# Rotary position embedding on one core: stores widened by ScalarE and issued by SyncE in place of casting stores from the software queue

## The chip, the cores and the metric

The kernel runs on 1 core of one Trainium2 chip. The metric is device time in microseconds for one launch; each kernel is run several times and the median is given. The engines named here are VectorE (DVE in the profile), ScalarE (ACT), GpSimd (POOL) and SyncE (SP). TensorE does nothing in this kernel. DMAs that GpSimd issues go through the software queue (q0 in the profile, "software_dynamic"); DMAs that SyncE issues go through a hardware queue (q1, "hardware_dynamic"). Both queues are served by the same 16 DMA engines of the core.

## The reference

```python
# x: (8, 2048, 16, 64) float32: batch, sequence, heads, head dimension
# cos, sin: (2048, 32) float32
x1, x2 = x[..., :32], x[..., 32:]
out1 = x1 * cos - x2 * sin
out2 = x1 * sin + x2 * cos
out = concatenate([out1, out2], axis=-1)      # float32
```

The cosines and sines depend on the position in the sequence alone and are shared by all batches and heads. The input and the output have 67.1 MB each. There are three multiplications or additions for each element of the output, so the kernel moves much and computes little.

## The kernel before

**Tiling.** A batch has 2048 positions. They are laid over 128 partitions, J = 16 consecutive positions to a partition, so that a partition holds 16 x 1024 elements of a batch: 64 KB of consecutive float32 in HBM. On the chip a batch is kept as float16, 32 KB a partition, in a tile `xt`. Five such tiles exist (`NBUF = 5`, line 27). There is one scratch tile `v` of the same size (line 31).

**Loads and stores.** `load` (lines 49 to 57) issues one DMA from GpSimd for a whole batch; it reads float32 and writes float16, so the DMA engines do the cast. `store` (lines 59 to 63) issues one DMA from GpSimd for a whole batch, which reads float16 and writes float32. Loads and stores of all batches therefore stand in one queue, and that queue is worked off in the order in which GpSimd issues them.

**The rotation.** `rotate` (lines 65 to 81) runs three VectorE operations over rows j0 to j1 of a batch. The first multiplies the halves of each head in exchanged order by the sines, of which the first half is negated, into `v` (line 73). The second multiplies `xt` by the cosines in place (line 79). The third adds `v` to `xt` in place (line 81). All operands are float16.

**The start.** Rows 0 and 1 of batch 0 (`JA = 2`) take another way: SyncE loads them as float32 into the tile `head` (line 36), and ScalarE narrows them into `xt` (line 84). SyncE then loads the sines and the cosines (lines 44 and 45). ScalarE turns them into float16 tables (lines 88 to 90). GpSimd issues the loads of batches 0 to 3 (line 83). Rows 0 and 1 are rotated first, and a store of row 0 alone (line 102, through line 100) goes out before the load of batch 4 (line 109). The order of these in the queue is fixed by hand with the `add_manual_dep` calls.

**The loop** (lines 116 to 128). For each batch, VectorE rotates the whole batch; GpSimd then issues its store, and then the load of the batch five further on, which first waits until the store has left the buffer.

**The end** (lines 129 to 147). The last batch is stored in three parts. Rows 0 to 8 go by the software queue (the DMA called `gate`, line 130), rows 9 to 13 too (line 132). Rows 14 and 15 are widened to float32 by ScalarE into `head` (line 140), and SyncE stores them (line 141) when `gate` has landed.

Of the kernel before, what the change touches and what calls it, by code (L numbers as in the profile page):

```python
# [1 line left out]

# [4 lines left out]


@with_exitstack  # L10
def kernel(
    ctx: ExitStack,
    tc: tile.TileContext,
    x: bass.AP,
    cos: bass.AP,
    sin: bass.AP,
    out: bass.AP,
):
    nc = tc.nc
    f16 = mybir.dt.float16  # L20
    f32 = mybir.dt.float32

    B, S, H, D = x.shape
    Dh = D // 2
    P = nc.NUM_PARTITIONS
    J = S // P
    NBUF = 5

    const_pool = ctx.enter_context(tc.tile_pool(name="rope_const", bufs=1))
    io_pool = ctx.enter_context(tc.tile_pool(name="rope_io", bufs=NBUF))  # L30
    tmp_pool = ctx.enter_context(tc.tile_pool(name="rope_tmp", bufs=1))

    JA = 2
    head = const_pool.tile([P, JA, H, D], f32)
    x0 = x[0].rearrange("(p j) h d -> p j (h d)", j=J)
    nc.sync.dma_start(  # L36
        out=head.rearrange("p j h d -> p (j h d)"),
        in_=x0[:, 0:JA, :].rearrange("p j f -> p (j f)"),
    )
    sin_f = const_pool.tile([P, J, Dh], f32)  # L40
    cos_f = const_pool.tile([P, J, Dh], f32)
    cos_h = const_pool.tile([P, J, Dh], f16)
    sin_h = const_pool.tile([P, J, D], f16)
    nc.sync.dma_start(out=sin_f, in_=sin.rearrange("(p j) d -> p j d", j=J))  # L44
    nc.sync.dma_start(out=cos_f, in_=cos.rearrange("(p j) d -> p j d", j=J))

    loads = []

    def load(b):
        xt = io_pool.tile([P, J, H, D], f16)  # L50
        j0 = JA if b == 0 else 0
        dma = nc.gpsimd.dma_start(  # L52
            out=xt[:, j0:J, :, :].rearrange("p j h d -> p (j h d)"),
            in_=x[b].rearrange("(p j) h d -> p j (h d)", j=J)[:, j0:J, :].rearrange("p j f -> p (j f)"),
        )
        loads.append(dma)
        return xt

    def store(b, xt, j0=0):
        return nc.gpsimd.dma_start(  # L60
            out=out[b].rearrange("(p j) h d -> p j (h d)", j=J)[:, j0:J, :].rearrange("p j f -> p (j f)"),
            in_=xt[:, j0:J, :, :].rearrange("p j h d -> p (j h d)"),
        )

    def rotate(xt, j0, j1):
        v = tmp_pool.tile([P, J, H, D], f16)
        n = j1 - j0
        js = slice(j0, j1)
        shape = [P, n, H, 2, Dh]
        sin_b = sin_h[:, js, :].rearrange("p j (e d) -> p j e d", e=2).unsqueeze(2).to_broadcast(shape)  # L70
        cos_b = cos_h[:, js, :].unsqueeze(2).to_broadcast([P, n, 2 * H, Dh])
        xe = xt[:, js, :, :].rearrange("p j h (e d) -> p j h e d", e=2)
        nc.vector.tensor_mul(  # L73
            out=v[:, js, :, :].rearrange("p j h (e d) -> p j h e d", e=2),
            in0=xe[:, :, :, ::-1, :],
            in1=sin_b,
        )
        xw = xt[:, js, :, :].rearrange("p j h (e d) -> p j (h e) d", d=Dh)
        nc.vector.tensor_mul(out=xw, in0=xw, in1=cos_b)  # L79
        xa = xt[:, js, :, :].rearrange("p j h d -> p (j h d)")  # L80
        nc.vector.tensor_add(out=xa, in0=xa, in1=v[:, js, :, :].rearrange("p j h d -> p (j h d)"))  # L81

    tiles = [load(b) for b in range(NBUF - 1)]
    nc.scalar.copy(  # L84
        out=tiles[0][:, 0:JA, :, :].rearrange("p j h d -> p (j h d)"),
        in_=head.rearrange("p j h d -> p (j h d)"),
    )
    nc.scalar.copy(out=sin_h[:, :, Dh:D], in_=sin_f)  # L88
    nc.scalar.mul(out=sin_h[:, :, 0:Dh], in_=sin_f, mul=-1.0)  # L89
    nc.scalar.copy(out=cos_h, in_=cos_f)  # L90
    rotate(tiles[0], 0, JA)
    def part(b, j0, j1):
        return (
            out[b].rearrange("(p j) h d -> p j (h d)", j=J)[:, j0:j1, :].rearrange("p j f -> p (j f)"),
            tiles[b][:, j0:j1, :, :].rearrange("p j h d -> p (j h d)"),
        )

    def store_rows(b, j0, j1):
        dst, src = part(b, j0, j1)
        return nc.gpsimd.dma_start(out=dst, in_=src)  # L100

    first = store_rows(0, 0, 1)
    tc.add_manual_dep(
        first.ins,
        loads[NBUF - 2].ins.name,
        mybir.DependencyInfo(mybir.DependencyClass.NoSync, mybir.DependencyReason.DATA),
        reason="order of the ring",
    )
    tiles.append(load(NBUF - 1))
    tc.add_manual_dep(  # L110
        loads[NBUF - 1].ins,
        first.ins.name,
        mybir.DependencyInfo(mybir.DependencyClass.NoSync, mybir.DependencyReason.DATA),
        reason="order of the ring",
    )
    for b in range(B):
        rotate(tiles[b], JA if b == 0 else 0, J)
        if b < B - 1:
            st = store(b, tiles[b], 1 if b == 0 else 0)
            if b == 0:  # L120
                tc.add_manual_dep(
                    st.ins,
                    first.ins.name,
                    mybir.DependencyInfo(mybir.DependencyClass.NoSync, mybir.DependencyReason.DATA),
                    reason="order of the ring",
                )
        if b + NBUF < B:
            tiles.append(load(b + NBUF))
    dst, src = part(B - 1, 0, 9)
    gate = nc.gpsimd.dma_start(out=dst, in_=src)  # L130
    dst, src = part(B - 1, 9, J - JA)
    rest = nc.gpsimd.dma_start(out=dst, in_=src)  # L132
    tc.add_manual_dep(
        rest.ins,
        gate.ins.name,
        mybir.DependencyInfo(mybir.DependencyClass.NoSync, mybir.DependencyReason.DATA),
        reason="order of the ring",
    )
    dst, src = part(B - 1, J - JA, J)
    nc.scalar.copy(out=head.rearrange("p j h d -> p (j h d)"), in_=src)  # L140
    end = nc.sync.dma_start(out=dst, in_=head.rearrange("p j h d -> p (j h d)"))
    tc.add_manual_dep(
        end.ins,
        gate.ins.name,
        mybir.DependencyInfo(mybir.DependencyClass.Sync, mybir.DependencyReason.DATA),
        reason="the last rows go out behind this part",
    )


# [1 line left out]
_INS = ['x', 'cos', 'sin']  # L151
_OUTS = [((8, 2048, 16, 64), 'float32')]


# [23 lines left out]
```

## Time and profile before

| What | Value |
|---|---|
| median of 3 runs | 316.88 us (316.84 to 317.36) |
| span of the profiled execution | 315.7 us |
| own time of the profiled execution | not listed; the median of the runs is 1.2 us above the span |
| VectorE busy | 209.1 us (66%), 27 instructions |
| ScalarE busy | 6.8 us (2%), 6 instructions |
| GpSimd busy | 9.9 us (3%), 22 instructions |
| software queue q0 | 2592 packets, 99.09 MB, 98.1% of 16 engines' span |
| hardware queue q1 | 576 packets, 2.62 MB, 2.3% |
| HBM read and written | 67.63 MB and 67.11 MB |
| a load of a full batch, issue to landing | 41.3 us (median of 7) |

How to read it: busy time is summed over the instructions of an engine; the share is that of the span. For a DMA queue, the share is the time that its packets took, over the span of all 16 DMA engines. A packet here is one row of one partition, and its size in the records is that of the side that is written: a full batch is 128 packets of 64 KB when it is stored and 128 packets of 32 KB when it is loaded. Each of the 16 engines moves 8 of the 128 rows. The time from issue to landing holds the waiting in the queue as well as the transfer. The trace also records each packet by itself, with its start, its duration and its queue; the text calls these the packet records.

The profile has a row of digits for the DMA engines, one for each fortieth of the span, where 9 means busy for 90% or more. The view by stretches gives, for a stretch of time, what each engine was busy, the DMA share and the GB/s written.

### The profile page before, as it was taken

How to read it: one execution, taken by the hardware profiler on the slowest of the kernel's cores; microseconds unless marked ns; L12 is line 12 of the kernel's file. 1: busy time of each engine (PE TensorE's matmuls, PEld its weight loads, DVE VectorE, ACT ScalarE, POOL GpSimd, SP SyncE). 2: the span in 40 equal slices, each digit the busy share in tenths (PEclk: the TensorE clock that was granted, in tenths of full speed). 3: DMA queues.
4: the chain of work that ended last, by engine and by line, in shares of the span. 5: the costliest groups of instructions: out<-in, count | busy, mean ns of one | idle time of the engine just before them, and what ended most of it. 6: DMA issues, size and time to landing. Idle time of an engine off the chain costs nothing.

```text
span 315.7 us, 122 instructions
## 1 busy us (share of the span) xinstructions
DVE 209.1 (66%) x27; ACT 6.8 (2%) x6; POOL 9.9 (3%) x22
## 2 busy tenths in 40 slices
DVE  0010699999999999999999999994009994000000
ACT  4100000000000000000000000000000002000000
POOL 3000100000000000001000000100000001000000
DMA  9899999999999989999999999999999999999998
GB/s 277 183 262 208 199 220 245 199 199 199 266 199 199 498 374 523 399 332 241 224 199 199 390 407 399 399 531 266 199 249 482 399 399 515 415 399 399 432 434 330
DMA packets 3168, 101.71 MB, mean 322 GB/s; under 512 B 352, under 2 KB 352, under 8 KB 736
## 3 DMA queue, kind: packets, MB, share of 16 engines
q0 software_dynamic: 2592, 99.09, 98.1%
q1 hardware_dynamic: 576, 2.62, 2.3%
HBM read 67.63 MB, written 67.11 MB: 427 GB/s over the span
## 4 chain that ended last, share of the span: by engine, by line
DVE 25%; DMA 22%; issue 18%; another core or an unknown queue 17%; POOL 1%; ACT 1%; SPq 0%; POOLq 0%; DVEq 0%; ACTq 0%
DMA xt<-in_x_dram 12%; DMA cos_f<-in_cos_dram 10%; DVE xt L79 8%; DVE xt L81 8%; DVE v L73 8%; ACT head L140 1%; POOL out_dram L60 1%; POOL xt L52 0%; ACT cos_h L90 0%; SPq L44 0%; SPq L36 0%; POOLq L52 0%; POOLq L60 0%; DVEq L73 0%
## 5 line engine op out<-in xcount | busy, mean ns | idle before, releaser
L73 DVE TENSOR_TENSOR v<-xt,sin_h 128x16384 f16<-128x16384 f16 (+2 forms) x9 | 69.7, 7744 | 36.8 <-DMA xt<-in_x_dram 20.7
L79 DVE TENSOR_TENSOR xt<-xt,cos_h 128x16384 f16<-128x16384 f16 (+2 forms) x9 | 69.7, 7744 | 17.5 <-ACT cos_h L90 17.2
L81 DVE TENSOR_TENSOR xt<-xt,v 128x16384 f16<-128x16384 f16 (+2 forms) x9 | 69.7, 7744 | 0.3
L52 POOL DMA_DIRECT2D xt<-in_x_dram x8 | 4.4, 557 | 111.1 <-DMA out_dram<-xt 110.3
L140 ACT CAST head<-xt 128x2048 f32<-128x2048 f16 x1 | 1.9, 1897 | 229.5 <-DVE xt L81 229.5
L60 POOL DMA_DIRECT2D out_dram<-xt x7 | 3.7, 535 | 63.9 <-DVE xt L81 63.9
L130 POOL DMA_DIRECT2D out_dram<-xt x1 | 0.5, 531 | 46.3 <-DVE xt L81 46.3
L84 ACT CAST xt<-head 128x2048 f16<-128x2048 f32 x1 | 1.9, 1897 | 3.6 <-DMA head<-in_x_dram 3.6
L100 POOL DMA_DIRECT2D out_dram<-xt x1 | 0.5, 541 | 33.5 <-DVE xt L81 33.5
L84 ACT ACT_TABLE_LOAD x1 | 1.3, 1283 | 0.7 <-PEq L162 0.7
L90 ACT CAST cos_h<-cos_f 128x512 f16<-128x512 f32 x1 | 0.6, 618 | 17.8 <-DMA cos_f<-in_cos_dram 17.8
L88 ACT CAST sin_h<-sin_f 128x512 f16<-128x512 f32 x1 | 0.6, 617 | 7.2 <-DMA sin_f<-in_sin_dram 7.2
L89 ACT ACTIVATE sin_h<-sin_f 128x512 f16<-128x512 f32 x1 | 0.6, 624 | 0.0
L132 POOL DMA_DIRECT2D out_dram<-xt x1 | 0.5, 531 | 0.0
L162 POOL MEMSET const-float32-0.0<- 128x1 f32 x1 | 0.1, 99 | 0.2 <-issue 0.2
L162 POOL MEMSET const-bfloat16-1.0<- 128x1 bf16 x1 | 0.1, 102 | 0.0
L162 POOL MEMSET const-float32-1.0<- 128x1 f32 x1 | 0.1, 99 | 0.0
L162 POOL MEMSET const-uint8-127<- 128x1 uint8 x1 | 0.1, 99 | 0.0
## 6 DMA issues: line engine op xcount, KB each, us to landing
xt<-in_x_dram POOLq DMA_DIRECT2D x7, 4096.0 KB, 41.3
out_dram<-xt POOLq DMA_DIRECT2D x1, 7680.0 KB, 61.6
out_dram<-xt POOLq DMA_DIRECT2D x1, 4608.0 KB, 42.4
xt<-in_x_dram POOLq DMA_DIRECT2D x1, 3584.0 KB, 22.3
out_dram<-xt POOLq DMA_DIRECT2D x1, 2560.0 KB, 47.9
head<-in_x_dram SPq DMA_DIRECT2D x1, 1024.0 KB, 4.8
out_dram<-head SPq DMA_DIRECT2D x1, 1024.0 KB, 8.4
out_dram<-xt POOLq DMA_DIRECT2D x1, 512.0 KB, 47.1
```

Source lines behind the costliest of these rows:

```text
L52: dma = nc.gpsimd.dma_start(out=xt[:, j0:J, :, :].rearrange("p j h d -> p (j h d)"), in_=x[b].rearrange("(p j) h d -> p j (h d)", j=J)[:, ...
L60: return nc.gpsimd.dma_start(out=out[b].rearrange("(p j) h d -> p j (h d)", j=J)[:, j0:J, :].rearrange("p j f -> p (j f)"), in_=xt[:, j0:J ...
L73: nc.vector.tensor_mul(out=v[:, js, :, :].rearrange("p j h (e d) -> p j h e d", e=2), in0=xe[:, :, :, ::-1, :], in1=sin_b,)
L79: nc.vector.tensor_mul(out=xw, in0=xw, in1=cos_b)
L81: nc.vector.tensor_add(out=xa, in0=xa, in1=v[:, js, :, :].rearrange("p j h d -> p (j h d)"))
L84: nc.scalar.copy(out=tiles[0][:, 0:JA, :, :].rearrange("p j h d -> p (j h d)"), in_=head.rearrange("p j h d -> p (j h d)"),)
L88: nc.scalar.copy(out=sin_h[:, :, Dh:D], in_=sin_f)
L89: nc.scalar.mul(out=sin_h[:, :, 0:Dh], in_=sin_f, mul=-1.0)
L90: nc.scalar.copy(out=cos_h, in_=cos_f)
L100: return nc.gpsimd.dma_start(out=dst, in_=src)
L130: gate = nc.gpsimd.dma_start(out=dst, in_=src)
L140: nc.scalar.copy(out=head.rearrange("p j h d -> p (j h d)"), in_=src)
```

## The change

Every store now goes the way of the last two rows before. The batch is cut into four quarters of four positions to a partition (`JQ = 4`, 4096 elements a partition). For each quarter VectorE runs the same three operations, with a scratch tile `v` of a quarter's size, of which there are two. ScalarE then copies the quarter from float16 into one of three float32 tiles `stage` (16 KB a partition), and SyncE stores that tile, 2 MB, with no cast in the DMA. A widening waits until the store of three quarters before has landed.

There are four batch buffers, not five. The loads stay on the software queue as they were, and they are the only DMAs there. The load of batch b + 4 is issued after the loop over the quarters of batch b, and it waits until ScalarE has read the last quarter of that batch.

The small first rotation of two rows, the store of row 0 ahead of the others, the split of the last batch in three parts, and all orders given by hand are gone. Rows 0 and 1 of batch 0 are still loaded by SyncE, now into the first `stage` tile, and narrowed by ScalarE; they are rotated with the rest of the first quarter.

```diff
-    NBUF = 5
+    NBUF = 4
+    JA = 2
+    JQ = 4
...
-    tmp_pool = ctx.enter_context(tc.tile_pool(name="rope_tmp", bufs=1))
+    tmp_pool = ctx.enter_context(tc.tile_pool(name="rope_tmp", bufs=2))
+    out_pool = ctx.enter_context(tc.tile_pool(name="rope_out", bufs=3))
...
+    stage = out_pool.tile([P, JQ, H, D], f32, name="stage")
+    head = stage[:, 0:JA, :, :]
+    nc.sync.dma_start(out=flat(head), in_=rows(x, 0, 0, JA))
...
-    def store(b, xt, j0=0):
-        return nc.gpsimd.dma_start(
...
-    rotate(tiles[0], 0, JA)
...
-    first = store_rows(0, 0, 1)
...
     for b in range(B):
-        rotate(tiles[b], JA if b == 0 else 0, J)
-        if b < B - 1:
-            st = store(b, tiles[b], 1 if b == 0 else 0)
...
+        xt = tiles[b]
+        for j0 in range(0, J, JQ):
+            js = slice(j0, j0 + JQ)
+            v = tmp_pool.tile([P, JQ, H, D], f16, name="v")
...
+            nc.vector.tensor_mul(out=xw, in0=xw, in1=cos_b)
+            xa = flat(xt[:, js, :, :])
+            nc.vector.tensor_add(out=xa, in0=xa, in1=flat(v))
+            stage = out_pool.tile([P, JQ, H, D], f32, name="stage")
+            nc.scalar.copy(out=flat(stage), in_=xa)
+            nc.sync.dma_start(out=rows(out, b, j0, j0 + JQ), in_=flat(stage))
         if b + NBUF < B:
             tiles.append(load(b + NBUF))
-    dst, src = part(B - 1, 0, 9)
-    gate = nc.gpsimd.dma_start(out=dst, in_=src)
...
-    nc.scalar.copy(out=head.rearrange("p j h d -> p (j h d)"), in_=src)
-    end = nc.sync.dma_start(out=dst, in_=head.rearrange("p j h d -> p (j h d)"))
```

Here `rows(t, b, j0, j1)` is the slice of rows j0 to j1 of batch b in HBM with one run of consecutive elements to a partition, and `flat(t)` is a tile seen as one run to a partition.

More of the change, by code (lines that the diff above doesn't have):

```diff
@@ L26, with rows, flat @@
     J = S // P
-    NBUF = 5
+    NBUF = 4
+    JA = 2
+    JQ = 4
     const_pool = ctx.enter_context(tc.tile_pool(name="rope_const", bufs=1))
     io_pool = ctx.enter_context(tc.tile_pool(name="rope_io", bufs=NBUF))
-    tmp_pool = ctx.enter_context(tc.tile_pool(name="rope_tmp", bufs=1))
[L33 to L39, printed above, removed]
+    tmp_pool = ctx.enter_context(tc.tile_pool(name="rope_tmp", bufs=2))
+    out_pool = ctx.enter_context(tc.tile_pool(name="rope_out", bufs=3))
+    def rows(t, b, j0, j1):
+        return t[b].rearrange("(p j) h d -> p j (h d)", j=J)[:, j0:j1, :].rearrange("p j f -> p (j f)")
+    def flat(t):
+        return t.rearrange("p j h d -> p (j h d)")
+    stage = out_pool.tile([P, JQ, H, D], f32, name="stage")
+    head = stage[:, 0:JA, :, :]
+    nc.sync.dma_start(out=flat(head), in_=rows(x, 0, 0, JA))
     sin_f = const_pool.tile([P, J, Dh], f32)
@@ L45 @@
     nc.sync.dma_start(out=cos_f, in_=cos.rearrange("(p j) d -> p j d", j=J))
-    loads = []
     def load(b):
-        xt = io_pool.tile([P, J, H, D], f16)
+        xt = io_pool.tile([P, J, H, D], f16, name="xt")
         j0 = JA if b == 0 else 0
[L52 to L56, printed above, removed]
-        return xt
-    def store(b, xt, j0=0):
-        return nc.gpsimd.dma_start(
[L61 to L87, printed above, removed]
+        nc.gpsimd.dma_start(out=flat(xt[:, j0:J, :, :]), in_=rows(x, b, j0, J))
+        return xt
+    tiles = [load(b) for b in range(NBUF)]
+    nc.scalar.copy(out=flat(tiles[0][:, 0:JA, :, :]), in_=flat(head))
     nc.scalar.copy(out=sin_h[:, :, Dh:D], in_=sin_f)
@@ L90 @@
     nc.scalar.copy(out=cos_h, in_=cos_f)
-    rotate(tiles[0], 0, JA)
[L92 to L100, printed above, removed]
-    first = store_rows(0, 0, 1)
[L103 to L115, printed above, removed]
-    for b in range(B):
-        rotate(tiles[b], JA if b == 0 else 0, J)
-        if b < B - 1:
-            st = store(b, tiles[b], 1 if b == 0 else 0)
[L120 to L126, printed above, removed]
+    for b in range(B):
+        xt = tiles[b]
+        for j0 in range(0, J, JQ):
+            js = slice(j0, j0 + JQ)
+            v = tmp_pool.tile([P, JQ, H, D], f16, name="v")
+            sin_b = (
+                sin_h[:, js, :]
+                .rearrange("p j (e d) -> p j e d", e=2)
+                .unsqueeze(2)
+                .to_broadcast([P, JQ, H, 2, Dh])
+            )
+            cos_b = cos_h[:, js, :].unsqueeze(2).to_broadcast([P, JQ, 2 * H, Dh])
+            xe = xt[:, js, :, :].rearrange("p j h (e d) -> p j h e d", e=2)
+            xw = xt[:, js, :, :].rearrange("p j h (e d) -> p j (h e) d", d=Dh)
+            nc.vector.tensor_mul(
+                out=v.rearrange("p j h (e d) -> p j h e d", e=2),
+                in0=xe[:, :, :, ::-1, :],
+                in1=sin_b,
+            )
+            nc.vector.tensor_mul(out=xw, in0=xw, in1=cos_b)
[4 more added lines that the diff above has]
+            nc.sync.dma_start(out=rows(out, b, j0, j0 + JQ), in_=flat(stage))
@@ L127 @@
         if b + NBUF < B:
             tiles.append(load(b + NBUF))
-    dst, src = part(B - 1, 0, 9)
-    gate = nc.gpsimd.dma_start(out=dst, in_=src)
[L131 to L140, printed above, removed]
@@ L141 @@
-    end = nc.sync.dma_start(out=dst, in_=head.rearrange("p j h d -> p (j h d)"))
[L142 to L147, printed above, removed]
 _INS = ['x', 'cos', 'sin']
```

## The prediction

> **What bounds the kernel now.** I read the page's transfer part first, because the kernel moves 134.7 MB and computes little.
>
> ```profile
> DMA  9899999999999989999999999999999999999998
> ...
> q0 software_dynamic: 2592, 99.09, 98.1%
> ...
> HBM read 67.63 MB, written 67.11 MB: 427 GB/s over the span
> ```
>
> The DMA engines are 90% busy or more in every slice but three, and the software queue's packets alone fill 98.1% of 16 engines' span. No idle time is left to remove. VectorE's 66% lies beneath. So a change matters only if it alters the engines' work, or if it leaves them empty. The stretches by stage say what one byte costs:
>
> ```profile
> core 0: us, DVE busy (x) ACT busy (x) POOL busy (x), PEclk, DMA share, GB/s
> ...
> 104.00:140.00 36.00, 35.86 (x5) 0.00 (x0) 0.53 (x1) 1.00 0.99 424
> 142.00:178.00 36.00, 35.86 (x5) 0.00 (x0) 1.20 (x3) 1.00 1.01 218
> ```
>
> The first stretch is stores alone, the second loads alone. GB/s counts what is written: a load writes float16, so 218 means 436 read. Either way the float32 side limits. The packet records agree: a full batch, load or store, takes 19.32 us (8 rows of 64 KB on each engine, 2.415 us a row). Then the groups by shape, for the engines that get new work:
>
> ```profile
> L73 DVE TENSOR_TENSOR v<-xt,sin_h 128x16384 f16<-128x16384 f16 x7 | 60.8, 8693 | 20.9 <-DMA xt<-in_x_dram 20.7
> ...
> L140 ACT CAST head<-xt 128x2048 f32<-128x2048 f16 x1 | 1.9, 1897 | 229.5 <-DVE xt L81 229.5
> ...
> L73 DVE TENSOR_TENSOR v<-xt,sin_h 128x2048 f16<-128x2048 f16 x1 | 1.2, 1224 | 15.9 <-ACT sin_h L89 15.9
> ...
> L88 ACT CAST sin_h<-sin_f 128x512 f16<-128x512 f32 x1 | 0.6, 617 | 7.2 <-DMA sin_f<-in_sin_dram 7.2
> ```
>
> **New compute, all beneath the transfers.** A quarter is 4096 elements a partition. VectorE: (8693-1224)/14336 = 0.521 ns per element, so 1224 + 2048 x 0.521 = 2291 ns; three operations with 0.02 us between are 6.93 us a quarter, 27.7 a batch (26.2 before). ScalarE: (1897-617)/1536 = 0.833 ns per element, 3.60 us a widening. A quarter's store is a quarter of 19.32, about 4.85 us; with its share of loads the engines need 9.7 us a quarter. Thus VectorE (6.93) and ScalarE (3.60) are faster than the transfers on average; neither adds to the sum while quarters wait in line.
>
> **Does the line run empty?** Three widened quarters can stand at SyncE's queue. VectorE never waits for them: it works in the batch buffer and has two v. Only ScalarE waits, for the store three quarters back; behind that wait stand the next widenings, SP's next store, and, for a batch's last quarter, POOL's load into that buffer. Nothing but loads stands on POOL. First 43 us: as before; batches land at 23 and 43, cos at 33.6, VectorE starts its second operation at 34.3, and the first widened quarter leaves at about 42.5. Then the two queues share. How, the cos rows show (stretch 6 to 31 us):
>
> ```profile
> q0 software_dynamic: 192, 5.31, 98.6%
> q1 hardware_dynamic: 189, 0.33, 4.0%
> ```
>
> Small table rows of q1 went one at a time between big load rows, never several in a turn. If store rows (16 KB) take turns with load rows (64 KB), one quarter goes out per batch that comes in, in 8 x (2.41 + 0.61) = 24 us. Loads land at about 66, 90 and 114; then load 5 waits for quarter 7's widening, so for store 4: about 156, 195, 234. Each time one or more quarters are waiting, so the engines stay full. At 234 some 16 stores are left, 78 us, while VectorE ends near 262 and the last store starts near 309: 47 us of cover. Fewer buffers cost nothing there: the load that comes later leaves the engines to a store. If SP's rows were served only after all load rows waiting, batches would land earlier and the sum would be the same.
>
> **The sum, against the profiled execution.** Its span is 315.7; its own time is not listed, so I put it at the median, 316.88, which is 1.2 above the span.
> - Removed and added store rows. Before, the last store (8 KB rows, float32 on both sides, SP's queue) took 0.306 us a row by its packet records, 26.8 GB/s an engine; the casting row runs at 27.2. For a 16 KB row that gives 0.603 (as the casting row) to 0.612 (two 8 KB rows); I take 0.607, a fixed piece per row. 256 rows an engine, about +0.9 (0 to +2.3).
> - Alternation. A 2 KB row between two load rows stretched the pitch from 2.086 to 2.204, 0.118, where it takes 0.080 among its like: +0.038 for the two turns. About 48 of 64 load rows get a store row beside them: +1.8 (0 to +3.6, as a store row's turn does not appear).
> - Semaphore rows: 35 DMAs of SP at 0.009 to 0.022, for some ten stores at 0.042 in q0: +0.2 (0 to +0.4).
> - The first 512 KB store goes. The load ahead of it, batch 3, lasted 20.04 rather than 19.32: -0.7 (0 to -1.2).
> - The head: SP issues the same three loads, POOL four loads, ScalarE the same four operations; the small rotation of two rows goes, but batch 0 lands before cos: 0. The tail: both kernels end on SP's store with engines full until then: 0.
> - No q0 store is issued from POOL any more (0.54 us each): hidden, 0. The loads' issue may be slow beside VectorE: 20 us of delay would change nothing, as the queued stores and the 47 us cover it.
>
> Sum +2.2: 319.1 us, +0.7%. About 0.2%, 0.6 us, can be told from no change.
>
> A rule that speaks against the change: the Trainium skill, "DMA: Bandwidth & Descriptors", section "Anatomy of one DMA — SWDGE (gpsimd) path", fits each DMA on the software path as about 2.0 us fixed plus its bytes at 436 GB/s. Were that paid singly by some 22 more DMAs the estimate would be 44 us more, 361. This trace shows full batches following each other at 19.32 us with no such gap while another was queued; so I leave it out.
>
> **Rivals.**
> 1. *Three buffers are too few* (slower). The views of issues and of stretch 306.8 to 311.4 speak for it:
>
> ```profile
> out_dram<-head SPq DMA_DIRECT2D x1, 1024.0 KB, 8.4
> ...
> q0 software_dynamic: 96, 1.97, 103.4%
> ```
>
> SP's store was issued at 306.43 and no q1 row moved in that stretch; 8 x 0.306 = 2.45 of the 8.4 is transfer, 5.95 is waiting. I think it stood behind rows of q0 already taken up; at the start q1's first row came 1.45 us after SP's issue, with q0 empty. If the wait were each store's own, one turn of a buffer is (3.60 + w + 4.86)/3 against 4.86: it decides from w = 6.1, just above 5.95. At 7.4, 0.43 us on each of some 22 stores with no load beside them: +9.5 on the forecast, 328.
> 2. *SP's rows get more turns* (slower). The last batch still needs 27.7 + 3.6 + 1.5 + 4.9 + 0.4, 38 us after its landing; beyond about 279 it sets the end. That needs five store rows per load row (landing near 290, end 328 of span): about 329. The cos rows speak against it.
> 3. *Not slower: a store row passes beside a load row.* A load row writes only half of what it reads, so the engine's write side is half idle in it. If some of the inserted 0.607 is hidden, the 48 insertions turn: the other terms, +0.4, are gone from 0.01 us hidden each. A third hidden: -0.2 x 48 = -10, with +0.4, 307; all hidden, 288. Against it: the new store reads as many bytes as it writes, so a read side that a load fills has no room for it; and the 2 KB rows cost more than their own time beside a load, not less. They write as the load does, though; a store row writes the other way, which no row here shows.
> 4. *Reading and writing HBM at once slows both.* From 43 us on some 145 us of mixed rows; at 3%, +4.4: 323.5. Before never mixes for long; its switches between load and store batches show no loss.
>
> **How the numbers follow.** Forecast 0.53 (own range 316.3 to 322); rival 1: 0.10; 2: 0.04; 3: 0.21; 4: 0.12. Faster: most of rival 3, 0.18. Within 0.2%: rest of rival 3 and the low end of the forecast, 0.12. Slower: 0.70. The range from 311 to 328 takes in the bounds of the terms, the start of rival 3, rival 4 and rival 1's example; its deeper cases are left out.
>
> **What would show it.** Right: DMA digits of 9 throughout; q0 near half its share; VectorE's work ended by about 262, ScalarE waiting mostly for stores; widenings near 3.6 us, VectorE's near 2.29; loads landing near 66, 90, 114, 156, 195, 234. Rival 1: DMA digits below 9 after the last load, SP's stores 9 us or more to landing there. Rival 2: last load after 280. Rival 3: total DMA time falls and shares pass 1.0 in mixed stretches. Rival 4: rows above 2.45 us in mixed stretches only. The forecast is wrong if mixed rows cost anything else than the sum of both, which carries most of the risk.

## The result, and the profile after

The changed kernel takes 319.93 us (median of 5 runs, 319.80 to 321.55), against 316.88 us before (316.84 to 317.36). The ratio is 1.0104, with a 95% interval from 1.0093 to 1.0116: about 3 us slower. The forecast was 319.1, slower.

The profiled execution of the changed kernel is the longest of its five: its span is 319.6 us, the others have 317.9 to 318.2. This matters below.

First the transfer part of the page after, the lines that were read first before. The digits are the busy share of the DMA engines in fortieths of the span; a queue's line gives packets, MB, and its share of the 16 engines' span.

```profile
DMA  9899998989989989998999998998999999999994
...
q1 hardware_dynamic: 5040, 68.68, 50.6%
q0 software_dynamic: 1152, 33.03, 48.3%
...
HBM read 67.63 MB, written 67.11 MB: 422 GB/s over the span
```

The load has moved as planned: the software queue fell from 98.1% to 48.3%, and SyncE's queue took the rest. Together they still fill 98.9% of the engines' span. The digits are as full as before, except in the last slice, where the digit is 4 and not 8. The packet records say the same: from 6 us until the first engine has moved its last row, the engines stand empty for 0.04 us each, all stretches together. The same bytes go at 422 GB/s rather than 427.

Next the groups of ScalarE and VectorE, as count, busy us, mean ns of one, and the idle time before them with its cause.

```profile
L88 ACT CAST stage<-xt 128x4096 f32<-128x4096 f16 x32 | 115.3, 3605 | 158.0 <-DMA out_dram<-stage 145.1
L79 DVE TENSOR_TENSOR v<-xt,sin_h 128x4096 f16<-128x4096 f16 x32 | 72.0, 2297 | 48.7 <-DMA xt<-in_x_dram 48.7
```

The new operations cost what the fits said (3605 against 3600 ns, 2297 against 2291 ns). ScalarE stood idle for 145 us behind stores. That is not a loss: it says that the queue of stores was full. The same is seen in the rhythm near the end, in the timeline (start, duration, engine, and in brackets the wait before it):

```profile
294.24 3.60 ACT L88 CAST stage<-xt 128x4096 f32<-128x4096 f16 x1 [1.26 <-DMA out_dram<-stage]
...
299.11 3.60 ACT L88 CAST stage<-xt 128x4096 f32<-128x4096 f16 x1 [1.26 <-DMA out_dram<-stage]
303.98 3.60 ACT L88 CAST stage<-xt 128x4096 f32<-128x4096 f16 x1 [1.27 <-DMA out_dram<-stage]
```

A store lands every 4.87 us, and each time ScalarE has waited for it. A quarter of the 19.32 us that a full batch took before is 4.83. So the new stores run at nearly, not quite, the old rate.

The chain that ended last shows how long a tile is away (start, duration, what):

```profile
263.84 10.86 DMA out_dram<-stage
...
274.79 3.61 ACT stage L88
278.42 10.86 DMA out_dram<-stage
```

From the end of a widening to the landing of its store are 10.86 us, and 10.86 + 3.61 + 0.1 is three times 4.86: the tile waits for the two stores ahead of it, then is stored. The chain names this DMA, ScalarE, DMA, but the turn is filled by transfers alone.

Last, two stretches by stage and the end (us, busy time and count by engine, clock, DMA share, GB/s written):

```profile
core 0: us, DVE busy (x) ACT busy (x) POOL busy (x), PEclk, DMA share, GB/s
...
67.00:115.00 48.00, 48.00 (x23) 7.21 (x2) 0.53 (x1) 1.00 0.99 255
243.00:315.00 72.00, 23.66 (x11) 48.22 (x14) 0.00 (x0) 1.00 1.01 431
316.00:319.00 3.00, 0.00 (x0) 0.00 (x0) 0.00 (x0) 1.00 0.04 16
```

The first is loads and stores mixed, the second stores alone; both are full. The third is the end: for 3 us the share is 0.04, less than one engine of sixteen at work. The queue line for 316.4 to 318.7 us has two store rows left and the four bytes that report the end:

```profile
q1 hardware_dynamic: 3, 0.03, 3.3%
```

The packet records show the rest. Fifteen engines end their last row between 315.2 and 315.8 us; the sixteenth ends four rows later, at 318.1. Before, all sixteen ended between 314.0 and 314.5. The late engine fell back between 54 and 68 us, when the first stores met load 2 (the load of batch 2, counted from 0): four of its load rows took up to 3.5 us instead of 2.4, and its load 2 ended at 68.7 where the others ended by 66.6. The records do not name an engine. But in every store outside the mixed stretches one last row trails the other fifteen, by 2.1 us up to 133 us, by 1.8 from 165 to 211 us, and by 2.3 from 245 us to the end, so it is taken to be the same engine. At the end it moved its four rows alone.

So the span's 3.9 us more fall into three parts. All sixteen engines are at work until 315.2 instead of 314.0 (+1.2). The last engine ends 2.9 instead of 0.5 us after that (+2.4). From there to the end of the span are 1.5 instead of 1.2 (+0.3). The four other executions, of which there are no packet records, are 1.4 to 1.7 us shorter; so most of the middle part is probably this execution's own.

### The profile page after: what moved, and what is told of

Read it like the earlier page. It is cut to its first block, busy times and chain, and to the rows that moved or that the text cites. A ratio compares the mean times of both kernels' runs of the same rounds, so it can differ in the third digit from the quotient of the medians.

```text
span 319.6 us, 306 instructions
## 1 busy us (share of the span) xinstructions
DVE 211.8 (66%) x96; ACT 120.2 (38%) x37; POOL 4.6 (1%) x12
## 3 DMA queue, kind: packets, MB, share of 16 engines
q0 software_dynamic: 1152, 33.03, 48.3%
## 4 chain that ended last, share of the span: by engine, by line
DMA 73%; ACT 13%; another core or an unknown queue 8%; DVE 2%; issue 0%; SPq 0%; ACTq 0%
DMA out_dram<-stage 63%; ACT stage L88 12%; DMA cos_f<-in_cos_dram 10%; DVE xt L84 1%; DVE xt L86 1%; ACT cos_h L63 0%; ACTq L88 0%; SPq L50 0%; SPq L45 0%
## 5 line engine op out<-in xcount | busy, mean ns | idle before, releaser
L88 ACT CAST stage<-xt 128x4096 f32<-128x4096 f16 x32 | 115.3, 3605 | 158.0 <-DMA out_dram<-stage 145.1
L79 DVE TENSOR_TENSOR v<-xt,sin_h 128x4096 f16<-128x4096 f16 x32 | 72.0, 2297 | 48.7 <-DMA xt<-in_x_dram 48.7
L84 DVE TENSOR_TENSOR xt<-xt,cos_h 128x4096 f16<-128x4096 f16 x32 | 72.0, 2297 | 6.2 <-ACT cos_h L63 6.2
L86 DVE TENSOR_TENSOR xt<-xt,v 128x4096 f16<-128x4096 f16 x32 | 72.0, 2298 | 0.0
L60 ACT CAST xt<-stage 128x2048 f16<-128x2048 f32 x1 | 1.9, 1897 | 3.7 <-DMA stage<-in_x_dram 3.7
```

Of the source, the lines that this page charges most:

```text
L60: nc.scalar.copy(out=flat(tiles[0][:, 0:JA, :, :]), in_=flat(head))
L79: nc.vector.tensor_mul(out=v.rearrange("p j h (e d) -> p j h e d", e=2), in0=xe[:, :, :, ::-1, :], in1=sin_b,)
L86: nc.vector.tensor_add(out=xa, in0=xa, in1=flat(v))
L88: nc.scalar.copy(out=flat(stage), in_=xa)
```

## The experiments

The theory is: the change leaves the DMA engines full, and the 3 us are a little more work per byte (smaller rows, alternation) and engines that end further apart. The rivals are: the missing fifth buffer; waits of the chain VectorE, ScalarE, SyncE; and a slowing of transfers where loads and stores mix. In brackets after a time stands the ratio to the kernel before, run on the same chip in the same round, with its interval.

### The buffer alone

```diff
-    NBUF = 5
+    NBUF = 4          # in the kernel before, nothing else
```

> The kernel before with four batch buffers instead of five, nothing else. Theory A (the buffers cost nothing as long as the queue holds a transfer): 316.5 to 317.5. Rival (the loss of 3 us is the missing fifth buffer): 319 to 321. If the single queue runs empty while a load waits for its store: each time 2 us or more, 320 to 330.

Measured: 317.67 us (1.0007, 0.9997 to 1.0016). The fifth buffer cost nothing to give up. Its line of DMA digits is as full as before:

```profile
DMA  9999999899899999999999999999999999999997
```

### Three batch buffers, four tiles

```diff
-    NBUF = 4
+    NBUF = 3
-    out_pool = ctx.enter_context(tc.tile_pool(name="rope_out", bufs=3))
+    out_pool = ctx.enter_context(tc.tile_pool(name="rope_out", bufs=4))
```

> The changed kernel with three batch buffers and four float32 tiles. Theory A (buffers only shift the loads, the last one by 10 to 20 us, and 47 us of cover remain): 319 to 321. Rival (the fifth buffer that went is part of the 3 us): one more missing costs at least as much again, 322 or more.

Measured: 320.04 us (1.0076, 1.0064 to 1.0088), that is no other than the changed kernel. Three batch buffers with four tiles do as well as four with three; each step alone was not run. The last load is issued at 224.3 us instead of 210.2, and the cover takes it.

### Two tiles

```diff
-    out_pool = ctx.enter_context(tc.tile_pool(name="rope_out", bufs=3))
+    out_pool = ctx.enter_context(tc.tile_pool(name="rope_out", bufs=2))
```

> The changed kernel with two float32 tiles instead of three. From its trace a tile comes back in 0.08 (landing to widening) + 3.61 + about 1.5 (issue to first row) = 5.2 us, against 4.86 for the one store that stands in between: 0.35 us lost with each of some 22 stores that run alone, +8, 326 to 330; DMA digits below 9 after the last load. If rows follow the issue quicker on a busy queue, 320 to 322. Rival of the prediction (each store waits 5.95 us of its own): 2.35 us on 22 stores, above 360.

Measured: 329.98 us (1.0395, 1.0377 to 1.0413), within the first expectation and far from the 360 of a store that waits 5.95 us of its own. The stretch of stores alone, and its timeline:

```profile
251.00:327.00 76.00, 25.32 (x12) 50.46 (x14) 0.00 (x0) 1.00 0.97 409
```

```profile
307.01 3.60 ACT L88 CAST stage<-xt 128x4096 f32<-128x4096 f16 x1 [1.30 <-DMA out_dram<-stage]
312.19 3.60 ACT L88 CAST stage<-xt 128x4096 f32<-128x4096 f16 x1 [1.57 <-DMA out_dram<-stage]
317.05 3.60 ACT L88 CAST stage<-xt 128x4096 f32<-128x4096 f16 x1 [1.25 <-DMA out_dram<-stage]
```

By the packet records the last 16 stores land 5.08 us apart on average, where three tiles gave 4.87. That is 0.2 us a store, less than the 0.35 expected, and some 3 us in all. The price has three parts, by the same records, for one engine and against the changed kernel: it stands empty for 3.7 us more, its load rows beyond 2.43 us add 2.5 (3.5 against 1.0), and its store rows beyond 0.62 us add 3.9 (4.1 against 0.2). Together 10.1, as measured. So the time was as expected, and the make-up of the price was not. Three tiles are enough and two are not.

### The transfers alone, mixed

```diff
-    for b in range(B): ...   # rotation, widening, store
+    nc.vector.memset(flat(stage), 0.0)      # three tiles, once
+    nc.sync.dma_start(out=rows(out, b, j0, j0 + JQ), in_=flat(stages[n % 3]))   # 32 times
```

> Leaves out all of VectorE's rotation and ScalarE's widening: three float32 tiles are set to zero once and stored again and again, with the same 8 loads on the software queue and the same 32 stores by SyncE, which wait for nothing. Theory A (transfers alone set the time of the changed kernel; alternation costs 0.01 us a pair): 317 to 319.5, pairs of a load and a store row at 3.03 us. Rival (waits of the chain VectorE, ScalarE, SyncE cost some of the 3 us): 315.5 to 316.5. Rival (mixing costs 0.038 a pair, as the prediction had it): pairs at 3.06 and 64 of them, 0.9 above the changed kernel.

Measured: 319.18 us (1.0047, 1.0032 to 1.0061). This run leaves out the rotation and the widening and stores zeros. The same transfers with no computing between them are 1.5 us slower than the kernel before, and 0.8 to 0.9 faster than the changed kernel and the run with three batch buffers. Its two stretches:

```profile
49.00:193.00 144.00, 0.00 (x0) 0.00 (x0) 1.58 (x3) 1.00 1.00 258
195.00:315.00 120.00, 0.00 (x0) 0.00 (x0) 0.00 (x0) 1.00 1.01 431
```

The mixed stretch is steady: by the packet records a load row starts every 3.03 us, with one store row between. 2.415 + 0.6075 are 3.022. A pair costs 0.008 more than its rows, not 0.038. The engines end within 0.6 us of each other. The schedule is not quite that of the changed kernel, as the first store rows move at 25.8 us here and at 49.6 there.

### The transfers alone, apart

The first try held one store only:

```diff
+            if n == 0:
+                tc.add_manual_dep(st.ins, loads[B - 1].ins.name, ...)
```

> Leaves out the same work as the run of transfers alone that mixes; here the first store waits until the last load has landed, so that loads run first and stores after, with one gap of about 2 us between. Theory A (alternation costs 0.01 a pair, 64 pairs): the mixed run less 0.6 plus the gap, so 1 to 2 above it if no engine lags there, and less if mixing makes one engine lag. Rival (alternation costs 0.038): the same as the mixed run or below. In the loads' part 2.413 us a row, in the stores' part 0.6075.

It is inconclusive: SyncE issued fourteen stores before the last load had landed, at the same times as in the mixed run, so loads and stores mixed from 26 us on. It took 319.20 us (1.0048), the mixed case a second time. The next try holds all:

```diff
-            if n == 0:
+            if True:
```

> Leaves out VectorE's rotation and ScalarE's widening, as the two runs of transfers alone; now every store waits for the last load, so that no store row stands beside a load row. One gap between, landing to first store row, of 1.5 to 2 us. Theory A (a pair costs 0.01 more than its two rows): 64 x 0.01 less and the gap more than the mixed run of 319.2, so 320.0 to 320.7. Rival (0.038 a pair, as predicted): 2.4 less and the gap more, 318.3 to 319.0. Rival 3 of the prediction (a row passes beside another): 325 or more, as mixing would have hidden time.

Measured: 320.65 us (1.0098, 1.0085 to 1.0111), 1.5 to 1.6 above the mixed run. The gap shows in the one digit of 6 in the middle:

```profile
DMA  9899999999999999999699999999999999999997
```

Load rows take 2.415 us here to the end and none is stretched, so in these two runs the stretched rows come with the stores. That is no rule: in the kernel before, load rows are stretched by some 0.15 us each near 52 and 72 us, and its first store row moves at 82.1. Against that, a store takes 4.91 us and not 4.86 in this kernel, where all engines start their stores together. Gap +1.5, pairs -0.5, stretched rows -1.2, slower stores 32 x 0.05 = +1.6: +1.4, near what was measured. So what mixing costs here, keeping loads and stores apart costs as well, besides the gap. Why its stores are slower is not shown.

### Row size

```diff
-    JQ = 4                                                    # eighths
+    JQ = 2
-    out_pool = ctx.enter_context(tc.tile_pool(name="rope_out", bufs=3))
+    out_pool = ctx.enter_context(tc.tile_pool(name="rope_out", bufs=6))
```

> The changed kernel in eighths of a batch: 2 positions a partition, six tiles of 8 KB a partition instead of three of 16, 64 stores of 8 KB rows. Theory A (the fixed piece per row): 512 rows at 0.306 instead of 256 at 0.6075, +1.2, 320.8 to 321.6. Rival (a fixed cost per DMA that shows, 0.1 or more): +3 and up. Rival (nothing per row): 319.5 to 320.3.

Measured: 321.79 us (1.0132, 1.0118 to 1.0145). That is 1.86 more than the changed kernel, and 1.75 more than the run with three batch buffers beside it on the same chip, for 256 more rows an engine (and 32 more DMAs): 0.007 us a row. Time alone does not part rows from DMAs here.

```diff
-    JQ = 4                                                    # halves
+    JQ = 8
-    NBUF = 4
+    NBUF = 3
-    ... name="rope_tmp", bufs=2   name="rope_out", bufs=3
+    ... name="rope_tmp", bufs=1   name="rope_out", bufs=2
```

> The changed kernel in halves of a batch: 8 positions a partition, 32 KB rows, 16 stores of 4 MB, two float32 tiles, three batch buffers, one v. Theory A (a fixed piece of about 0.005 us a row): 128 rows of 1.21 instead of 256 of 0.6075, -0.7 to -0.9; a tile comes back in 0.08 + 7.2 + 1.5 = 8.8, less than the 9.7 of the other tile's store, so no gap: 318.8 to 319.5. Rival (two tiles are too few here too): 16 x 0.5 and up, 326 or more. Rival (nothing per row): 319.7 to 320.3.

Measured: 321.79 us (1.0117, 1.0088 to 1.0147), with single runs from 319.77 to 323.66. None of the three expectations holds. A row of 32 KB costs 1.21 us, as expected, and the stores follow each other every 9.68 us. But load rows beside such stores are stretched to 3.3 us and more, in all 4.0 us an engine in the profile, which is of the longest run. Why, these runs do not tell; the row term cannot be read from this kernel.

### Small rows on the software queue

```diff
     def store(b, xt, j0=0):            # in the kernel before
-        return nc.gpsimd.dma_start(out=... [:, j0:J, :] ..., in_=xt[:, j0:J, :, :] ...)
+        return [nc.gpsimd.dma_start(out=... [:, max(j0, k):k + 4, :] ..., in_=xt[:, max(j0, k):k + 4, :, :] ...)
+                for k in range(0, J, 4)]
```

> The kernel before, five buffers, all stores cast on the software queue, but each batch's store cut into four DMAs with 16 KB rows. Theory A (a 16 KB row has a fixed piece, 0.607 us against 0.603 of a quarter of a 64 KB row, whatever the queue): +0.8 to +1.3, 317.7 to 318.2. Rival (the hardware queue or the meeting of two queues is what costs, not the row): 316.7 to 317.2. Rival (each DMA has a fixed cost of its own that shows): 21 more DMAs at 0.1 or more, 319 or above.

Measured: 322.47 us (1.0126 without the longest run, 1.0086 to 1.0167), single runs from 318.43 to 324.67; the profile is of the longest. A casting 16 KB row takes 0.6075 us as well (a store every 4.86 us): the piece belongs to the row, not to the queue or the cast. The total, though, is above the first expectation: in the profile the three loads after the first cut stores are stretched, in all 4.6 us an engine, mostly in the last row or two of a load. That is near the third expectation in size and not in kind, as the stores follow each other without a gap. The run of 318.43 has no room for such a loss, so the stretching differs from run to run.

### Where the engines part

```diff
+            if b == 0 and j0 == 0:
+                tc.add_manual_dep(st.ins, loads[NBUF - 1].ins.name, ...)
```

> The changed kernel, with the first store held until the first four loads have landed (about 82 us), so that no store row stands beside load 2 and load 3. Theory A (of the 3 us lost, some 2 are one DMA engine that falls 2.1 us behind between 54 and 68 us, where the first stores meet load 2, and that keeps the lag to the end; all else is the row terms): load 2 and 3 at 2.42 us a row on all engines, last rows of all engines within 1 us, 317.3 to 318.7 us. Theory B (the lag has nothing to do with the first meeting of the two queues): 319.5 to 320.5. Theory C (alternation itself costs, rows lost everywhere): two loads of eight pairs fewer, 319.3 to 319.9.

Measured: 319.97 us (1.0078, 1.0065 to 1.0091). Here SyncE issued the three other stores of batch 0 ahead of the held one, so stores met load 2 at 52.2 us all the same, and this run does not tell theories A and B apart as meant. It still shows something: no engine fell back at load 2 (all ended it between 65.6 and 66.2 us), one was late at load 6 (199.9 against 198.4), the last rows ended 1.3 us apart, and the time is that of the changed kernel. So a lag that begins at load 2 is not needed for 320 us.

```diff
-            if b == 0 and j0 == 0:
+            if b == 0:
```

> The changed kernel with all four stores of batch 0 held until the first four loads have landed (the earlier try held one store only, and SyncE issued the three others ahead of it). No store row beside loads 2 and 3: these at 19.3 to 19.6 us each. Theory A (a lag of one engine that begins where the queues first meet is most of what lies between transfers alone, 319.2, and the changed kernel, 319.9): 318.7 to 319.3, and last rows of all engines within 1 us. Theory B (engines drift apart wherever the queues meet, so the lag comes at loads 4 to 7 as well): 319.7 to 320.5.

Measured: 322.27 us (1.015, 1.0137 to 1.0163). Both theories missed, as the hold cost more than it could show. The stores could not be issued before load 3 had landed, and then ScalarE's next widening and the load behind it came late. The wait and the late issue in the timeline:

```profile
88.26 3.61 ACT L90 CAST stage<-xt 128x4096 f32<-128x4096 f16 x1 [30.77 <-DMA out_dram<-stage]
92.16 0.53 POOL L58 DMA_DIRECT2D xt<-in_x_dram  x1 [88.68 <-ACT stage L90]
```

By the packet records the engines stand empty for 1.6 us after 81.1, until the first store row at 82.7. The load is issued at 92.2 us, its first row moves at 98.3, and only the three stores in the queue bridge that. Store rows beyond 0.62 us add 1.0 us an engine, against 0.2 in the changed kernel. The last rows ended 0.8 us apart, but a kernel with another loss in it cannot tell what the parting is worth. What it does tell: with the DMA engines full, idle time is paid in full. The 1.6 us and the 0.8 more of slow store rows make 2.4, and the run is 2.3 longer than the changed kernel.

### The first small store

```diff
-    first = store_rows(0, 0, 1)        # in the kernel before
...
-            st = store(b, tiles[b], 1 if b == 0 else 0)
+            st = store(b, tiles[b])
```

> The kernel before without its first store of 512 KB: row 0 of batch 0 goes out with the rest of the batch. Theory A (that store disturbs the load ahead of it; the prediction took 0.7 us from it): -0.5 to -0.9 against the kernel before. Theory B (the last rows of the first loads are stretched in any case, as the changed kernel shows the same sum of stretched rows without that store): within 0.3 of the kernel before.

Measured: 317.81 us (1.0008, 0.9999 to 1.0017). The time is that of theory B. The stretched load rows sum to 0.97 us an engine before, 0.96 without that store, and 1.0 in the changed kernel. The packet records show why nothing is saved. In the kernel before, the last row of load 3, just ahead of the small store, takes 2.8 to 3.0 us on every engine. Without that store it takes its 2.43, and the last row of load 4, now just ahead of the first store, takes 3.0 to 4.0. With four buffers it is the last row of load 2. The slow row goes with whichever store comes first, small or large.

## Why the prediction was right, and where it was not

It forecast slower by 2.2 us and it was slower by 3.05 at the medians, 2.4 to 2.5 by the ratios of its near copies (one store held, and three batch buffers). The mechanism was right: transfers set the time before and after, nothing of the new compute shows, and the line never runs empty. That the size came out as close as it did is partly luck: of the terms below, one was 1.4 us too large, one took off 0.7 us that was not there to save, and one of about 0.9 us was put at nothing.

- **Compute beneath the transfers**: right. VectorE's work ended near 267 us (262 expected); the first widened quarter left at 44.8 (42.5 expected). Loads landed for most engines near 66, 91, 115, 161, 200 and 239, against 66, 90, 114, 156, 195 and 234.
- **Row against row**: right. One store row per load row in the mixed stretch; the queues' turns do go by the row here. So rival 2, more turns for SyncE's rows, did not come: the last load ended near 239 us, not after 280.
- **Store rows, +0.9, and semaphore rows, +0.2**: right within what can be told. 0.607 was taken for a row, 0.6075 measured with the semaphore row in it. The kernel before has 88 store rows an engine, the changed one 256; at the 0.007 of the eighths the 168 more give +1.2.
- **Alternation, +1.8**: mis-sized by a misreading. A pair costs about 0.008, so some 48 make +0.4. The 2.086 us taken for the pitch of load rows alone is not what the packet records of the kernel before have. Those rows of 28 KB follow each other at 2.114 us alone and at 2.204 with a table row between; the difference is 0.090, of which 0.080 is the table row itself. So the same row, read rightly, says 0.010 a pair: +0.5, and a forecast of 317.8.
- **The first 512 KB store goes, -0.7**: failed. Taking that store out of the kernel before changes nothing, and the changed kernel has the same sum of stretched rows. The slow last row ahead of that store was read as an effect of this small store; in the kernel before and its variants it comes ahead of the first store, whichever that is.
- **The tail, 0**: failed. "Both kernels end on SP's store with engines full until then" holds for fifteen engines. One ends 2.3 us after the others in the profile, and 1.3 and 1.8 us lie between the first and the last engine in the two near copies, against 0.5 before. The chain, set against transfers alone, costs 0.8 to 0.9 us.
- **Rival 1, too few tiles**: not so with three; with two, yes, at +10. Of the 5.95 us of the last store before, 5.1 were the wait for its first row (issued at 306.4, first row at 311.5 us). The first store of the changed kernel met such a wait again (issued at 44.8, first rows from 49.6 to 50.4 us), later ones with rows in the queue did not. That it is a wait behind rows already taken fits, but was not tested. The 1.45 us read at the start are 1.0 by the packet records (issued at 0.74, first row at 1.73).
- **Rival 3, a row beside another**: not so. 3.03 us is the sum of both rows, and keeping loads and stores apart costs no more than its gap and its slower stores.
- **Rival 4, mixing slows**: not in the changed kernel's steady stretch. In the halves, in the cut stores and with two tiles load rows beside stores were stretched by 3.5 to 4.6 us in all. So there is something of the kind, and what it depends on was not found.
- **The rule set beside the sum**, 44 us: its fit is for DMAs of the software path, and the DMAs that were added go by SyncE's queue. The eighths, with 32 more of those, took 1.75 us longer in all.

With the sizes measured: rows +1.2, alternation +0.4, and the engines' parting with the end of the span +0.9, sum +2.5. The first two agree with the +1.5 of transfers alone, and with the packet records: the packet times of an engine (the sum of all packets' times over 16, less the stretches in which more than 16 were in flight) are 1.2 us longer in the changed kernel's profile than before, 1.3 and 1.5 in the near copies. What makes engines part is not shown, nor that it belongs to the change: variants of the kernel before, in which the software queue carries the loads and all stores but the last, also ended 1.2 (four buffers), 1.7 (no small store) and 3.1 us (cut stores) apart in their profiles.

No version tried beats the kernel before. Its engines are at work from 2 to 314.0 us, and the bytes are fixed.

## What to carry to other kernels

Where the page's transfer part is full from end to end, moving a cast from the DMA to an idle engine need gain nothing: here a 16 KB row took 0.6075 us with the cast and without. Look instead at bytes, at the number of rows (0.007 us each here), and at anything that lets the queue run empty. An engine's long wait for DMA is no loss when the landings come at the transfer's own rhythm: compare the two before you add buffers. A term read from one slow row next to an event should be tested on the event before it enters a sum. And a small difference of two pitches, multiplied by 48, deserves a second reading of both.

## What was not expected of the hardware

In the profile of the changed kernel a DMA engine that fell back kept its lag: 2.1 us lost near 60 us were, at 1.8 to 2.3, still there 250 us later, and set the end. A store's pace differs from kernel to kernel: 4.86 us per 2 MB behind a mixed stretch, 4.91 where all engines started their stores together after a wait; why was not tried. A new transfer on SyncE's queue waited some 5 us for its first row while load rows were moving, at 44.8 us, while later ones, with rows in the queue, followed each other without a gap. And the last load row ahead of the first store was slow, by 0.4 to 1.6 us, in the kernel before and in its variants with four buffers and without the small store.
